# GLA decay factors: the second product in rounded parts stacked in 98 rows, both directions in one tile

## The chip, the cores and the metric

The kernel runs on one core of one Trainium2 chip, as one launch. The metric is the device time in microseconds (us) of that launch. The engines named below are PE (matrix products), ACT (functions, copies and casts), DVE (elementwise work), POOL and SP, which issues nearly all transfers. Each engine works through its own instructions in a fixed order and waits for the others by semaphores.

## The reference

The reference is one layer of a hybrid diffusion backbone, for 128 context tokens and 256 latent tokens with 2048 channels. The part that the change touches is the decay of the gated linear attention (GLA): four heads, key width 128, two directions, chunks of 64 tokens. Cut to that part:

```python
lr_f, lr_b = ...            # two slices of h @ w_in, 16 columns each
la_f = heads(jax.nn.log_sigmoid((lr_f @ lw['w_a2_fwd'] + lw['b_a_fwd']).astype(jnp.float32)) / GLA_TAU, GLA_DK)
la_b = heads(jax.nn.log_sigmoid((lr_b @ lw['w_a2_bwd'] + lw['b_a_bwd']).astype(jnp.float32)) / GLA_TAU, GLA_DK)
...
b = jnp.cumsum(lc, axis=3)                 # in a chunk, along the direction
q_in = qc * jnp.exp(b)
k_in = kc * jnp.exp(-b)
k_out = kc * jnp.exp(total - b)
```

The product with `w_a2` is called the second product here: a row of 16 low-rank factors, and a bias, give the decay logits z of a token in 512 key channels per direction. From `q_in`, `k_in` and `k_out` follow the attention inside the chunks, the running state and the outputs. Around this stand the input projections, a Fourier branch, per-channel gates, an output projection and a SwiGLU feed-forward part.

## The kernel before

All 384 tokens are handled together, T = 384 columns, with channels in the partitions. A product of full precision is made of rounded parts: each operand is split into `hi`, its rounded copy (type F32R), and `lo`, the rest, and three products hi-hi, hi-lo and lo-hi are added in PSUM (`gemm`, L249). Weights come in tiles of 128x1024 (`raw`, two buffers); a cast on ACT (L220, `whi`) and a subtraction on DVE (L221, `wlo`) split each tile, into one of four buffers. One tile serves half a projection: 24 matmuls of 384 columns. `grab` (L240) takes the oldest split tile and at once queues the load and the split of another, so three half projections lie between a split and its use. `proj` (L258) does a projection in two halves, and after each half it calls `step(side)`.

The side work of the gate stage is two generators (`side`, L761), advanced by one `yield` each after every half projection. One is `gla` (L583), the attention, head by head: 14 yields a head. The other is `ada_rest` (L519), a matrix-vector product on DVE that loads 512 KB (`adaw`) and does two instructions (`adacc`, L530) per yield. The order on PE, ACT, DVE and POOL is as written in the program; the order of SP's transfers is chosen by a scheduler.

Of a head's 14 steps the first five matter here:

- transposes of k (`kr`, L598);
- `z` of direction 0, and its logarithms;
- `z` of direction 1, and its logarithms;
- `bT` and `sx` of direction 0 (the cumulative sums, products with the triangular matrix `tri`);
- `bT` and `sx` of direction 1.

The logits z of a direction are three plain fp32 matmuls (L614) of 33 rows (32 low-rank factors of both directions, and a row of ones for the bias; the other direction's 16 rows of `a2` are zero) by 128 columns. Then log-sigmoid: ACT takes |z| (L618), exp(-|z|) (L619) and ln(1 + .) (L620), DVE subtracts that from min(z, 0) (L621), ACT rounds the result (`lah`, L624) and DVE takes the rest (`lal`, L625).

The 33-row operand `lr` is made in three moves. The first low-rank products are made in plain fp32, in four row groups (`lrprod`, L409). Those are summed by a selection matrix `sel32` (`plr`, L750), and ACT copies the 32 rows (L752). `a2` and the constants are loaded at the end of the first stage (L496, L497), into a buffer of x that is then free.

Of the kernel before, what the change touches and what calls it, by code (L numbers as in the profile page):

```python
# [11 lines left out]
F32 = mybir.dt.float32  # L12
# [8 lines left out]
P = 128  # L21
# [21 lines left out]
C_MASK = 512  # L43
C_SELS = 640
C_SELR = C_SELS + 2
C_SEL32 = C_SELR + 64
HC, HL = TC // 2 + 1, TL // 2 + 1
HT = HC + HL
C_CR = C_SEL32 + 32
C_CT = C_CR + 129 + 129 + 128  # L50
C_LT = C_CT + 2 * HC
NC = C_LT + 2 * 2 * HL
# [2 lines left out]
def _constants():  # L55
    c = np.zeros((P, NC), np.float32)
    j = np.arange(P)[:, None]
    i = np.arange(P)[None, :]
    same = (j // CH) == (i // CH)
    c[:, 0:128] = (same & (j <= i)) / TAU  # L60
    c[:, 128:256] = (same & (j >= i)) / TAU
    c[:, 256:384] = (j > i) / TAU
    c[:, 384:512] = (j < i) / TAU
    jc, ic = j % CH, np.arange(CH)[None, :]
    c[:, C_MASK : C_MASK + CH] = jc <= ic
    c[:, C_MASK + CH : C_MASK + 2 * CH] = jc >= ic
    r = np.arange(P)
    for k in range(2):
        c[:, C_SELS + k] = (r % 32) == k
        c[:, C_SELR + 32 * k + k] = 1.0  # L70
    c[:, C_SEL32 : C_SEL32 + 32] = (r[:, None] % 32) == np.arange(32)[None, :]
# [21 lines left out]
def tile_step(ctx: ExitStack, tc: tile.TileContext, a, o):  # L93
# [26 lines left out]
    sel32 = const.tile([P, 32], F32, name="sel32")  # L120
    selr = const.tile([P, 64], F32, name="selr")
    tmp1 = const.tile([P, 1], F32, name="tmp1")

# [188 lines left out]
    with ExitStack() as s:  # L312
# [38 lines left out]
        load_w(1)  # L351
        wlr = pa.tile([P, KT, 32], F32, name="wlr")
        SP.dma_start(wlr, a["w_lr"])
        SP.dma_start(sel32, a["consts"][:, C_SEL32 : C_SEL32 + 32])
# [84 lines left out]
        for kb in range(KT):  # L439
# [48 lines left out]
            if kb:  # L488
# [2 lines left out]
                pe_x(3)  # L491
                flushes[3]()
                prev = new
        cgt = actp.tile([P, 8, T], F32, tag="C_lo", name="cg")
        cg = cgt.rearrange("p a b -> p (a b)")
        SP.dma_start(cg[:, 0:640], a["consts"][:, 0:640])  # L496
        SP.dma_start(cg[0:33, 768:1792], a["a2"])  # L497
        lrmm, lrflush = lrprod(KT - 4)
        lrmm()
        lrflush(cgt[:, 6, :])  # L500
        push()
        qk = actp.tile([P, 8, T], F32, tag="C_hi", name="qk")
# [61 lines left out]

        return qk[:, h:8:4, t * P : (t + 1) * P]

    a2 = cg[0:33, 768:1792]
    rate = [1.0]
    ada_gen = ada_rest((2, 3, 4))
    ada = paced(ada_gen, rate)  # L570
    with ExitStack() as s:
        pg = s.enter_context(tc.tile_pool(name="pg", bufs=1))
        tri = pg.tile([P, 512], F32R, name="tri")
        mask = pg.tile([P, 2, CH], U32, name="mask")
        ss = pg.tile([P, 3, 4], F32, name="ss")

# [6 lines left out]
        def gla():  # L583
            def split2(tags, src):
                out = [pg.tile([P, src.shape[1], src.shape[2]], F32R, tag=t, name="part") for t in tags]
                split_act(*out, src)
                return out
# [6 lines left out]
            for h in range(NH):  # L594
# [11 lines left out]
                    SP.dma_start(s0[d], a["s0"][d, h])  # L606
                yield
                qin, kin, kcr, kout, dec = [], [], [], [], []
                lasplit = []
                for d in range(2):  # L610
                    z = pss.tile([P, 3, P], F32, tag="side", name="z")
                    for t in range(3):
                        c0 = d * 512 + h * P
                        PE.matmul(  # L614
                            z[:, t, :], lr[0:33, t * P : (t + 1) * P], a2[0:33, c0 : c0 + P], start=True, stop=True,
                        )
                    la = pg.tile([P, 3, P], F32, tag=f"la{d}", name="la")
                    ACT.activation(la, z, AF.Abs)  # L618
                    ACT.activation(la, la, AF.Exp, scale=-1.0)  # L619
                    ACT.activation(la, la, AF.Ln, bias=1.0)  # L620
                    DVE.scalar_tensor_tensor(la, z, 0.0, la, op0=ALU.min, op1=ALU.subtract)  # L621
                    lah = pg.tile([P, 3, P], F32R, tag=f"lah{d}", name="lah")
                    lal = pg.tile([P, 3, P], F32R, tag=f"lal{d}", name="lal")
                    ACT.copy(lah, la)  # L624
                    DVE.tensor_sub(lal, la, lah.bitcast(F32))  # L625
                    lasplit.append((lah, lal))
                    yield
                for d in range(2):
                    lah, lal = lasplit[d]


                    bT = pss.tile([P, T], F32, tag="side", name="bT")
                    for t in range(3):
                        for j, l in enumerate((lah, lal)):
                            PE.matmul(
                                bT[:, t * P : (t + 1) * P], l[:, t, :], tri[:, d * P : (d + 1) * P],
                                start=j == 0, stop=j == 1,
                            )
                    sx = pss.tile([P, 2, P], F32, tag="side", name="sx")
                    for j, l in enumerate((lah, lal)):  # L640
                        PE.matmul(
                            sx, tri[:, (2 + d) * P : (3 + d) * P], l[:, 0 : 2 + d : 1 + d, :], start=j == 0, stop=j == 1,
                        )
# [24 lines left out]
                    yield  # L668
# [35 lines left out]
                ap = split2(("la0", "la1"), att)  # L704
                yield
                qp = [split2((f"lah{d}", f"lal{d}"), qin[d].rearrange("p (t i) -> p t i", t=3)) for d in range(2)]
# [43 lines left out]
        PE.matmul(plr[0:32, :], sel32, cgt[:, 6, :], start=True, stop=True)  # L750
        lr = cgt[0:33, 7, :]
        ACT.copy(lr[0:32, :], plr[0:32, :])  # L752
        POOL.memset(lr[32:33, :], 1.0)
        for i in range(4):
            proj(psm, hT, keep(kT, i), ada)
        DVE.tensor_copy(tri, cg[:, 0:512])
        DVE.tensor_copy(mask, cg[:, C_MASK : C_MASK + 2 * CH].rearrange("p (a b) -> p a b", a=2))

        gl = gla()

# [549 lines left out]
```

## Time and profile before

| what | value |
|---|---|
| three timed runs | 2064.86, 2067.26, 2067.55 us; median 2067.26 |
| the profiled execution, its own time | 2063.03 us |
| its span, first to last instruction | 2061.3 us |
| mean granted clock of PE | 0.994 |
| busy: PE, DVE, ACT, POOL | 2031.1, 1273.7, 780.5, 45.4 us |
| transfers | 373.64 MB, mean 181 GB/s |

A row of a group or of the timeline names the line of the program, the engine, the operation, and `out<-in` by the names of the tiles. Rows of the timeline begin with the start and the length in microseconds; in brackets stand the idle time of the engine before the row and what ended it. PE records overlap, since matmuls are pipelined: the time that a matmul takes of PE is read from start to start. A plain fp32 matmul is recorded as two.

### The profile page before, as it was taken

How to read it: one execution, taken by the hardware profiler on the slowest of the kernel's cores; microseconds unless marked ns; L12 is line 12 of the kernel's file. 1: busy time of each engine (PE TensorE's matmuls, PEld its weight loads, DVE VectorE, ACT ScalarE, POOL GpSimd, SP SyncE). 2: the span in 40 equal slices, each digit the busy share in tenths (PEclk: the TensorE clock that was granted, in tenths of full speed). 3: DMA queues.
4: the chain of work that ended last, by engine and by line, in shares of the span. 5: the costliest groups of instructions: out<-in, count | busy, mean ns of one | idle time of the engine just before them, and what ended most of it. 6: DMA issues, size and time to landing. Idle time of an engine off the chain costs nothing.

```text
span 2061.3 us, 30173 instructions
## 1 busy us (share of the span) xinstructions
PE 2031.1 (99%) x12250; PEld 1959.8 (95%) x12250; DVE 1273.7 (62%) x1662; ACT 780.5 (38%) x1161; POOL 45.4 (2%) x52
## 2 busy tenths in 40 slices
PE   8999999999999999998999999999999999999997
PEld 5779999999999999988999999999999999999996
DVE  5669787888667787867444545453545454544346
ACT  3233555454346554445333223222222222232234
POOL 0000000000000000023000000000000000000001
PEclk9999999999999999999999999999999999999999
DMA  9977666767546685632444444443444444433332
GB/s 387 352 274 262 196 223 226 243 206 263 203 154 224 237 294 179 193 124 74 162 145 142 154 153 143 143 151 126 143 143 154 144 151 146 149 127 123 123 133 82
DMA packets 112167, 373.64 MB, mean 181 GB/s; under 512 B 13627, under 2 KB 32251, under 8 KB 107932
## 3 DMA queue, kind: packets, MB, share of 16 engines
q1 hardware_dynamic: 111164, 370.54, 52.5%
q8 instruction: 96, 1.57, 0.3%
q10 hardware_dynamic: 864, 1.18, 0.2%
q14 instruction: 43, 0.35, 0.1%
HBM read 358.04 MB, written 13.63 MB: 180 GB/s over the span
## 4 chain that ended last, share of the span: by engine, by line
PE 96%; DVE 2%; issue 0%; DMA 0%; ACT 0%; SPq 0%; DVEq 0%; ACTq 0%
PE pmm L253 66%; PE pdn L253 18%; PE pv L387 3%; PE pf L253 2%; PE pgm L370 2%; PE px L405 1%; DVE yE L1205 0%; PE po L592 0%; DMA Clo<-in_xT 0%; PE pr L538 0%; PE z L614 0%; DVE z L1068 0%; PE dl L592 0%; PE pgm L468 0%; DVE z L1062 0%
## 5 line engine op out<-in xcount | busy, mean ns | idle before, releaser
L253 PE MATMUL pmm<-A_hi,whi 128*128 128x384 f32 x2480 | 833.3, 336 | 0.0
L253 PE MATMUL pmm<-A_hi,wlo 128*128 128x384 f32 x2480 | 829.1, 334 | 0.0
L253 PE MATMUL pmm<-A_lo,whi 128*128 128x384 f32 x2480 | 829.0, 334 | 0.0
L221 DVE TENSOR_TENSOR wlo<-raw,whi 128x1024 fp32r<-128x1024 f32 x433 | 529.1, 1224 | 433.1 <-ACT whi L220 424.1
L220 ACT CAST whi<-raw 128x1024 fp32r<-128x1024 f32 x436 | 457.6, 1050 | 616.9 <-PE pmm L253 212.0
L253 PEld LDWEIGHTS pmm<-A_hi,whi 128*128 128x128 f32 x2480 | 465.6, 188 | 4.8 <-issue 1.6
L253 PEld LDWEIGHTS pmm<-A_lo,whi 128*128 128x128 f32 x2480 | 465.7, 188 | 0.0
L253 PEld LDWEIGHTS pmm<-A_hi,wlo 128*128 128x128 f32 x2480 | 465.6, 188 | 0.0
L530 DVE SCALAR_TENSOR_TENSOR adacc<-adaw,spad,adacc 128x1024 f32<-128x1024 f32 x240 | 297.0, 1279 | 0.9 <-DMA adaw<-in_w_ada 0.7
L253 PE MATMUL pdn<-hid_hi,whi 128*128 128x384 f32 x704 | 235.2, 334 | 0.0
L253 PE MATMUL pdn<-hid_hi,wlo 128*128 128x384 f32 x704 | 235.1, 334 | 0.0
L253 PE MATMUL pdn<-hid_lo,whi 128*128 128x384 f32 x704 | 235.1, 334 | 0.0
L253 PEld LDWEIGHTS pdn<-hid_hi,whi 128*128 128x128 f32 x704 | 132.2, 188 | 0.4 <-issue 0.4
L253 PEld LDWEIGHTS pdn<-hid_lo,whi 128*128 128x128 f32 x704 | 132.2, 188 | 0.0
L253 PEld LDWEIGHTS pdn<-hid_hi,wlo 128*128 128x128 f32 x704 | 132.2, 188 | 0.0
L279 ACT CAST hid_hi<-hfE 128x384 fp32r<-128x384 f32 x44 | 22.6, 513 | 160.4 <-DVE hfE L1132 160.4
L1132 DVE TENSOR_TENSOR hfE<-sg,pmm 128x384 f32<-128x384 f32 x44 | 24.4, 555 | 81.1 <-PE pmm L253 80.5
L1124 ACT ACTIVATE sg<-pmm 128x384 f32<-128x384 f32 x44 | 21.7, 492 | 133.3 <-PE pmm L253 133.3
L1149 DVE TENSOR_TENSOR Blo<-Blo,pdn 128x384 f32<-128x384 f32 x72 | 39.5, 553 | 46.6 <-PE pdn L253 46.6
L1149 DVE TENSOR_TENSOR Bhi<-Bhi,pdn 128x384 f32<-128x384 f32 x72 | 39.2, 550 | 34.1 <-PE pdn L253 33.9
L253 PE MATMUL pmm<-o_hi,whi 128*128 128x384 f32 x128 | 42.8, 335 | 0.0
L253 PE MATMUL pmm<-o_lo,whi 128*128 128x384 f32 x128 | 42.8, 334 | 0.0
(297 smaller groups left out, 1575.6 us busy)
## 6 DMA issues: line engine op xcount, KB each, us to landing
adaw<-in_w_ada SPq DMA_DIRECT2D x128, 512.0 KB
raw<-in_w_g SPq DMA_DIRECT2D x88, 512.0 KB
raw<-in_w_u SPq DMA_DIRECT2D x88, 512.0 KB
raw<-in_w_d SPq DMA_DIRECT2D x88, 512.0 KB
slab<-in_w_ada SPq DMA_DIRECT2D x32, 1024.0 KB
raw<-in_w_gate SPq DMA_DIRECT2D x64, 512.0 KB
raw<-in_w_in SPq DMA_DIRECT2D x44, 512.0 KB
raw<-in_w_out SPq DMA_DIRECT2D x32, 512.0 KB
```

The lines of the kernel that those rows point to most:

```text
L220: ACT.copy(hi, raw)
L221: eng.tensor_sub(lo, raw, hi.bitcast(F32))
L253: PE.matmul(dst, w[wi][:, k * n + n0 : k * n + n0 + P], x[xi][:, k0 + k, :], start=first and k == 0 and j == 0, stop=last and k == kts - 1 ...
L279: ACT.copy(hi, src)
L370: PE.matmul(pgv[q : q + 32, :], spad[:, k, :], slab[k // (KT // 2)][:, k % (KT // 2), :], start=k < 4, stop=k >= KT - 4,)
L387: PE.matmul(pv[2 * t + g], hT[x_][:, kb, t * P : (t + 1) * P], w_[:, g * 512 : (g + 1) * 512], start=kb == 0 and j == 0, stop=kb == KT - 1 ...
L405: PE.matmul(px, w_[:, u * P : (u + 1) * P], hT[x_][:, kb, :], start=j == 0, stop=j == 2)
L530: DVE.scalar_tensor_tensor(acc[:, c, :], w, spad[:, k, c : c + 1], acc[:, c, :], op0=ALU.mult, op1=ALU.add,)
L1124: ACT.activation(sgs[j], p, AF.Silu)
L1132: DVE.tensor_mul(hf, sgs.pop(j), p)
L1149: DVE.tensor_add(acc(k), acc(k), p)
```

## The change

- **The operands of the second product** become rounded parts. `lr` has 98 rows: 32 rows of hi, the same 32 rows again, 32 rows of lo, and two rows of ones. `a2` has 98 rows too: hi, lo, hi, then the bias as hi and lo. One matmul in F32R over 98 rows adds the three products and the bias.
- **Side by side**: the columns of `a2` are laid out by head, direction, channel, so that one matmul of 256 columns gives both directions of a head. Three matmuls a head take the place of six.
- **One tile per head** holds the decays of both directions: |z| in two instructions (512 and 256 columns, by PSUM tile), the other functions in one of 768 columns, the subtraction in two, `lah` and `lal` in one each. z of both directions stands in the second step of a head and the logarithms stand in the third. Before, each direction had its z and its logarithms in one step. The number of steps is the same.
- **Preparation**: the selection matrix gives three copies of the 32 rows (96 columns). Ten transfers (constants, selection, eight pieces of `a2`) go to the tiles of `la`, `lah` and `lal` in place of two to `cg`. Before the gate stage two ACT and four DVE instructions make the parts of `a2`; one more on DVE makes the lo rows of `lr`. `tri` moves to `cg`.

```diff
+        cg = actp.tile([P, 8 * T], F32R, tag="C_lo", name="cg")
+        tri, a2, lr = cg[:, 0:512], cg[0:98, 768:1792], cg[0:98, 7 * T : 8 * T]
+        part = pg.tile([P, 512], F32R, name="a2part")
+        raw3 = [pg.tile([P, 768], F32, tag=t, name="raw3") for t in ("la", "lah", "lal")]
+        SP.dma_start(raw3[0][:, 0:640], a["consts"][:, 0:640])
+        SP.dma_start(raw3[0][:, 640:736], a["consts"][:, C_SEL3 : C_SEL3 + 96])
+        for c in range(2):
+            src = a["a2"][:, 512 * c : 512 * c + 512]
+            for n in range(3):
+                SP.dma_start(raw3[1 + c][32 * n : 32 * n + 32, 0:512], src[0:32])
+            SP.dma_start(raw3[1 + c][96:98, 0:512], src[32:33].to_broadcast([2, 512]))
...
-                lasplit = []
+                z = [pss.tile([P, n, 2, P], F32, tag="side", name="z") for n in (2, 1)]
+                for t in range(3):
+                    PE.matmul(
+                        z[t // 2][:, t % 2], lr[:, t * P : (t + 1) * P], a2[:, h * 2 * P : (h + 1) * 2 * P],
+                        start=True, stop=True,
+                    )
+                yield
+                la = pg.tile([P, 3, 2, P], F32, tag="la", name="la")
+                lap = [la[:, 0:2], la[:, 2:3]]
+                for n in range(2):
+                    ACT.activation(lap[n], z[n], AF.Abs)
+                ACT.activation(la, la, AF.Exp, scale=-1.0)
+                ACT.activation(la, la, AF.Ln, bias=1.0)
+                for n in range(2):
+                    DVE.scalar_tensor_tensor(lap[n], z[n], 0.0, lap[n], op0=ALU.min, op1=ALU.subtract)
+                lah, lal = (pg.tile([P, 3, 2, P], F32R, tag=t, name=t) for t in ("lah", "lal"))
+                split_act(lah, lal, la)
+                yield
                 for d in range(2):
-                    z = pss.tile([P, 3, P], F32, tag="side", name="z")
-                    for t in range(3):
-                        c0 = d * 512 + h * P
-                        PE.matmul(
-                            z[:, t, :], lr[0:33, t * P : (t + 1) * P], a2[0:33, c0 : c0 + P], start=True, stop=True,
-                        )
-                    la = pg.tile([P, 3, P], F32, tag=f"la{d}", name="la")
-                    ACT.activation(la, z, AF.Abs)
-                    ACT.activation(la, la, AF.Exp, scale=-1.0)
-                    ACT.activation(la, la, AF.Ln, bias=1.0)
-                    DVE.scalar_tensor_tensor(la, z, 0.0, la, op0=ALU.min, op1=ALU.subtract)
-                    lah = pg.tile([P, 3, P], F32R, tag=f"lah{d}", name="lah")
-                    lal = pg.tile([P, 3, P], F32R, tag=f"lal{d}", name="lal")
-                    ACT.copy(lah, la)
-                    DVE.tensor_sub(lal, la, lah.bitcast(F32))
-                    lasplit.append((lah, lal))
-                    yield
-                for d in range(2):
-                    lah, lal = lasplit[d]
...
-        PE.matmul(plr[0:32, :], sel32, cgt[:, 6, :], start=True, stop=True)
-        lr = cgt[0:33, 7, :]
-        ACT.copy(lr[0:32, :], plr[0:32, :])
-        POOL.memset(lr[32:33, :], 1.0)
+        PE.matmul(plr[0:96, :], raw3[0][:, 640:736], qk[:, 7, :], start=True, stop=True)
+        ACT.copy(lr[0:96], plr[0:96, :])
+        DVE.tensor_sub(lr[64:96], plr[64:96, :], lr[64:96].bitcast(F32))
+        POOL.memset(lr[96:98].bitcast(F32), 1.0)
         for i in range(4):
             proj(psm, hT, keep(kT, i), ada)
...
+        for c in range(2):
+            dst = a2.rearrange("p (h d j) -> p d h j", d=2, j=P)[:, c]
+            raw, up = (x.rearrange("p (h j) -> p h j", j=P) for x in (raw3[1 + c][0:98, 0:512], part[0:98]))
+            ACT.copy(up, raw)
+            DVE.tensor_scalar_mul(dst, up.bitcast(F32), coef[0:98, 1:2])
+            DVE.scalar_tensor_tensor(dst, raw, coef[0:98, 0:1], dst.bitcast(F32), op0=ALU.mult, op1=ALU.add)
```

More of the change, by code (lines that the diff above doesn't have):

```diff
@@ L45 @@
 C_SELR = C_SELS + 2
-C_SEL32 = C_SELR + 64
+C_COEF = C_SELR + 64
+C_SEL3 = C_COEF + 2
 HC, HL = TC // 2 + 1, TL // 2 + 1
 HT = HC + HL
-C_CR = C_SEL32 + 32
+C_CR = C_SEL3 + 96
 C_CT = C_CR + 129 + 129 + 128
@@ L70, in _constants @@
         c[:, C_SELR + 32 * k + k] = 1.0
-    c[:, C_SEL32 : C_SEL32 + 32] = (r[:, None] % 32) == np.arange(32)[None, :]
+    rest = ((r >= 32) & (r < 64)) | (r == 97)
+    c[:, C_COEF] = rest
+    c[:, C_COEF + 1] = np.where(rest, -1, 1)
+    c[:, C_SEL3 : C_SEL3 + 96] = (r[:, None] % 32) == (np.arange(96) % 32)[None, :]
     jj = np.arange(129)[None, :]
@@ L119, in tile_step @@
     msx = const.tile([P, 3], F32, name="msx")
-    sel32 = const.tile([P, 32], F32, name="sel32")
+    coef = const.tile([P, 32], F32, name="coef")
     selr = const.tile([P, 64], F32, name="selr")
@@ L353, in tile_step @@
         SP.dma_start(wlr, a["w_lr"])
-        SP.dma_start(sel32, a["consts"][:, C_SEL32 : C_SEL32 + 32])
+        SP.dma_start(coef[:, 0:2], a["consts"][:, C_COEF : C_COEF + 2])
         SP.dma_start(bgate, a["b_gate"])
@@ L493, in tile_step @@
                 prev = new
[L494 to L497, printed above, removed]
+        qk = actp.tile([P, 8, T], F32, tag="C_hi", name="qk")
         lrmm, lrflush = lrprod(KT - 4)
         lrmm()
-        lrflush(cgt[:, 6, :])
+        lrflush(qk[:, 7, :])
         push()
-        qk = actp.tile([P, 8, T], F32, tag="C_hi", name="qk")
         vr = [actp.tile([P, 3, 1024], F32R, tag=t, name="vr") for t in ("B_hi", "B_lo")]
@@ L565, in on @@
         return qk[:, h:8:4, t * P : (t + 1) * P]
-    a2 = cg[0:33, 768:1792]
     rate = [1.0]
@@ L572, in tile_step @@
         pg = s.enter_context(tc.tile_pool(name="pg", bufs=1))
-        tri = pg.tile([P, 512], F32R, name="tri")
+        cg = actp.tile([P, 8 * T], F32R, tag="C_lo", name="cg")
[9 more added lines that the diff above has]
+            SP.dma_start(raw3[1 + c][96:98, 0:512], src[32:33].to_broadcast([2, 512]))
         mask = pg.tile([P, 2, CH], U32, name="mask")
@@ L635, in gla @@
                             PE.matmul(
-                                bT[:, t * P : (t + 1) * P], l[:, t, :], tri[:, d * P : (d + 1) * P],
+                                bT[:, t * P : (t + 1) * P], l[:, t, d], tri[:, d * P : (d + 1) * P],
                                 start=j == 0, stop=j == 1,
@@ L641, in gla @@
                         PE.matmul(
-                            sx, tri[:, (2 + d) * P : (3 + d) * P], l[:, 0 : 2 + d : 1 + d, :], start=j == 0, stop=j == 1,
+                            sx, tri[:, (2 + d) * P : (3 + d) * P], l[:, 0 : 2 + d : 1 + d, d], start=j == 0, stop=j == 1,
                         )
@@ L703, in gla @@
                 kp = [split2((f"koh{d}", f"kol{d}"), kout[d]) for d in range(2)]
-                ap = split2(("la0", "la1"), att)
+                apt = pg.tile([P, 2, 3, P], F32R, tag="la", name="ap")
+                ap = [apt[:, 0], apt[:, 1]]
+                split_act(*ap, att)
                 yield
-                qp = [split2((f"lah{d}", f"lal{d}"), qin[d].rearrange("p (t i) -> p t i", t=3)) for d in range(2)]
+                qpt = [pg.tile([P, 2, 3, P], F32R, tag=t, name="qp") for t in ("lah", "lal")]
+                qp = [[q[:, d] for q in qpt] for d in range(2)]
+                for d in range(2):
+                    split_act(*qp[d], qin[d].rearrange("p (t i) -> p t i", t=3))
                 sp = [split2((f"s0h{d}", f"s0l{d}"), s0[d]) for d in range(2)]
@@ L749, in tile_step @@
         plr = pss.tile([P, T], F32, tag="side", name="plr")
-        PE.matmul(plr[0:32, :], sel32, cgt[:, 6, :], start=True, stop=True)
-        lr = cgt[0:33, 7, :]
-        ACT.copy(lr[0:32, :], plr[0:32, :])
-        POOL.memset(lr[32:33, :], 1.0)
+        PE.matmul(plr[0:96, :], raw3[0][:, 640:736], qk[:, 7, :], start=True, stop=True)
+        ACT.copy(lr[0:96], plr[0:96, :])
+        DVE.tensor_sub(lr[64:96], plr[64:96, :], lr[64:96].bitcast(F32))
+        POOL.memset(lr[96:98].bitcast(F32), 1.0)
         for i in range(4):
             proj(psm, hT, keep(kT, i), ada)
-        DVE.tensor_copy(tri, cg[:, 0:512])
-        DVE.tensor_copy(mask, cg[:, C_MASK : C_MASK + 2 * CH].rearrange("p (a b) -> p a b", a=2))
+        DVE.tensor_copy(tri, raw3[0][:, 0:512])
+        DVE.tensor_copy(mask, raw3[0][:, C_MASK : C_MASK + 2 * CH].rearrange("p (a b) -> p a b", a=2))
+        for c in range(2):
[4 more added lines that the diff above has]
+            DVE.scalar_tensor_tensor(dst, raw, coef[0:98, 0:1], dst.bitcast(F32), op0=ALU.mult, op1=ALU.add)
         gl = gla()
```

## The prediction

> **What bounds the kernel now.** I read the page first: span, busy shares, the chain that ended last.
>
> ```profile
> span 2061.3 us, 30173 instructions
> PE 2031.1 (99%) x12250; PEld 1959.8 (95%) x12250; DVE 1273.7 (62%) x1662; ACT 780.5 (38%) x1161; POOL 45.4 (2%) x52
> PE 96%; DVE 2%; issue 0%; DMA 0%; ACT 0%; SPq 0%; DVEq 0%; ACTq 0%
> ```
>
> TensorE is nearly always busy and carries 96% of the chain, so time taken off PE's stream shortens the span unless a new wait fills the hole. The change lies in the gate stage, 203 to 481 us, so I asked for the windows next, then for the waits between 140 and 440 us.
>
> ```profile
> 203.00:481.00 278.00, 278.00 (x1794) 269.11 (x1792) 227.44 (x293) 145.15 (x251) 1.86 (x6) 1.00 0.68 222
> ACT whi L220 <- DMA raw<-in_w_gate: 45.7, 17, 4.7
> ```
>
> The window's columns are length, then busy time of PE, PEld, DVE, ACT and POOL, then granted clock, DMA share, GB/s. PE is busy for all 278 us at full clock: no helper work of the attention heads makes it wait today. DVE is busy 227 of 278 us, ACT 145. ACT's largest wait here is for weight tiles; it matters below because a cast of such a tile comes to stand ahead of the decay work.
>
> **Part 1: the second product on PE.** The timeline of PE, the start of each row first:
>
> ```profile
> 203.70 0.33 PE L253 MATMUL pmm<-A_hi,whi 128*128 128x384 f32 x1
> ...
> 207.16 0.34 PE L253 MATMUL pmm<-A_hi,wlo 128*128 128x384 f32 x1
> 207.43 0.93 PE L614 MATMUL z<-cg 33*128 33x128 f32 x6
> ...
> 208.75 0.33 PE L253 MATMUL pmm<-A_hi,wlo 128*128 128x384 f32 x1
> ```
>
> From 203.70 to 207.16 lie 20 steps of the projection: 3.46 / 20 = 0.173 us each. From 207.16 to 208.75 are 1.59 us, of which three steps (0.52) are projection, so one z block costs PE 1.07 us: three plain fp32 matmuls, each recorded as two, and a slow return to the rounded stream. There are two per head and four heads, together 8.56 us.
>
> The new block is three matmuls per head of 256 columns in rounded fp32 with 98 rows. The trace has none with 98 rows; the nearest is a po block, the same type, width and count with 128 rows:
>
> ```profile
> 257.66 0.34 PE L253 MATMUL pmm<-A_hi,wlo 128*128 128x384 f32 x1
> 257.83 0.52 PE L592 MATMUL po<-vr,part 128*128 128x256 f32 x3
> 258.19 0.34 PE L253 MATMUL pmm<-A_hi,whi 128*128 128x384 f32 x1
> ```
>
> 0.53 less one step is 0.36 us. The far bounds are twice that row (0.72) and the old cost of both directions (2.14, no gain); I take 0.36, since only the row count differs. Saved: 4 x (2.14 - 0.36) = 7.1 us.
>
> The selection product plr keeps its two fp32 passes but loads 96 columns instead of 32:
>
> ```profile
> L750 PEld LDWEIGHTS plr<-cg,sel 128*32 128x32 f32 x2 | 0.1, 108 | 0.2 <-issue 0.2
> L614 PEld LDWEIGHTS z<-cg 33*128 33x128 f32 x48 | 5.9, 187 | 2.0 <-issue 2.0
> ```
>
> Two loads grow by at most 187 - 108 = 79 ns: 0 to 0.16 us, I take 0.1. The other matmuls (bT, sx, at, po) keep count, width and type. PE's own gain is 7.0 us.
>
> **Part 2: the chain from z to the cumulative sums.** Before, z of direction 0, z of direction 1, bT of 0 and bT of 1 stand in four successive steps, a step being half a projection (24 matmuls). The logarithms of a direction are made in the step of its z, so two half projections lie between them and their bT. The built order of the new kernel has z of both in the first step, the logarithms of both in the second, bT of 0 in the third: two half projections cover a chain twice as wide. In ACT's order the chain now also stands behind the weight cast (whi, L220) of the next half projection, where it stood ahead of it. ACT and DVE, head 0 before:
>
> ```profile
> 207.54 0.58 ACT L772 ACTIVATE gz<-pmm,bgate 128x384 f32<-128x384 f32 x1 [2.74 <-PE pmm L253]
> 208.40 0.49 ACT L618 ACTIVATE la<-z 128x384 f32<-128x384 f32 x1 [0.28 <-PE z L614]
> 208.91 1.28 ACT L619 ACT_TABLE_LOAD   x1
> 210.20 0.53 ACT L619 ACTIVATE la<-la 128x384 f32<-128x384 f32 x1
> 210.75 1.28 ACT L620 ACT_TABLE_LOAD   x1
> 212.04 0.53 ACT L620 ACTIVATE la<-la 128x384 f32<-128x384 f32 x1
> 213.19 0.51 ACT L624 CAST lah<-la 128x384 fp32r<-128x384 f32 x1 [0.62 <-DVE la L621]
> 213.61 1.05 ACT L220 CAST whi<-raw 128x1024 fp32r<-128x1024 f32 x1
> ```
>
> ```profile
> 212.60 0.56 DVE L621 SCALAR_TENSOR_TENSOR la<-z,la 128x384 f32<-128x384 f32 x1 [6.54 <-ACT la L620]
> 213.74 0.56 DVE L625 TENSOR_TENSOR lal<-la,lah 128x384 fp32r<-128x384 f32 x1 [0.58 <-ACT lah L624]
> ```
>
> Widths by slope: on ACT a cast goes from 0.51 us (384) to 1.05 (1024), 0.84 ns a column; on DVE 0.56 (384) to 1.28 (1024), 1.13 ns a column by the first row below.
>
> ```profile
> L530 DVE SCALAR_TENSOR_TENSOR adacc<-adaw,spad,adacc 128x1024 f32<-128x1024 f32 x93 | 115.2, 1279 | 0.4 <-DMA adaw<-in_w_ada 0.2
> 278.37 0.49 ACT L618 ACTIVATE la<-z 128x384 f32<-128x384 f32 x1 [0.28 <-PE z L614]
> 278.90 0.53 ACT L619 ACTIVATE la<-la 128x384 f32<-128x384 f32 x1
> ```
>
> The last two rows are head 1: there the exponential follows the absolute value with no table load, so heads 1 to 3 pay one load, head 0 two. In the new order, from the start of the last projection matmul before z (207.16 in head 0) as zero: gz starts at 0.38; whi at 0.86 (successive instructions overlap by 0.1); absolute value of 512 columns at 1.82 (0.60), of 256 at 2.32 (0.39), ending at 2.71; exponential of 768 (0.53 + 384 x 0.84 ns = 0.85) 2.74 to 3.59; load to 4.88; logarithm to 5.74; on DVE two subtractions (0.70 and 0.42) to 6.8; cast lah (0.84) 6.83 to 7.67; lal (0.56 to 1.0; I take 0.96) to 8.65. PE comes to bT this way:
>
> ```profile
> 217.67 0.34 PE L253 MATMUL pmm<-A_hi,wlo 128*128 128x384 f32 x1
> 217.85 0.22 PE L635 MATMUL bT<-tri,lah 128*128 128x128 f32 x1
> 217.91 0.27 PE L635 MATMUL bT<-tri,lal 128*128 128x128 f32 x1
> ```
>
> bT's second matmul, which reads lal, stands 0.24 us behind the last projection matmul: 0.36 + 48 x 0.173 + 0.24 = 8.91. In heads 1 to 3 the operand is there at 8.65, a quarter of a microsecond ahead; I put 0.1 us of stall on each (0 to 0.4). In head 0 the second load adds 1.28: ready at 9.93, or up to 0.4 later where whi's tile lands late (below): a stall of 1.0 to 1.6, I take 1.4. Together 1.7 us. Queued behind the waiting bT on PE is the whole stream of projections; nothing runs past it.
>
> The Trainium skill (page "ScalarE: Activation LUTs", section "What ACT_TABLE_LOAD costs") speaks against this margin: a switch costs the 1283 ns load plus about 1380 ns of drain. Here the load of 210.75 starts 0.02 us after the exponential ended and the logarithm starts 0.01 us after the load, so the trace shows no drain. By the page the chains would be 1.38 us longer for each load, two in head 0 and one in the others, the stall 4.2 + 3 x 1.2 = 7.8 in place of 1.7, and the gain gone; by the row the sum stands.
>
> Hidden elsewhere: eight table loads go, on an engine that is half idle. DVE loses five small instructions and no longer sits 6.54 us ahead of the first subtraction, since two adacc and a wlo now stand before it; they end near 3.2 on the scale above, before the 5.77 at which it is wanted. The preparation of a2 (two ACT copies of 512 columns near 0.6; four DVE instructions near 0.4 to 0.7; 2.4 us on DVE) falls at 199 us in front of weights that PE wants two or three half projections later; if that cover were gone it would cost those 2.4 us. The 0.56 us at most that lo of lr takes on DVE at 165 us is hidden the same way.
>
> **Part 3: the queue of SP at the start.** Two loads become ten: constants, selection, eight pieces of a2. They stand ahead of the fourth half projection's weights.
>
> ```profile
> 144.26 0.33 SPq L192 DMA_DIRECT2D raw<-in_w_in  x1
> 149.46 7.18 SPq L192 DMA_DIRECT2D raw<-in_w_in  x3
> ...
> 135.79 1.58 SPq L497 DMA_DIRECT2D cg<-in_a  x1
> L851 SPq DMA_DIRECT2D wr<-in_w_br_four x24: 620/621/737, 520.9 to 545.4; - x24
> 153.97 1.05 ACT L220 CAST whi<-raw 128x1024 fp32r<-128x1024 f32 x1 [4.46 <-DMA raw<-in_w_in]
> 164.50 0.83 PE L750 MATMUL plr<-cg,sel 128*32 128x384 f32 x2
> 166.17 0.33 SPq L192 DMA_DIRECT2D raw<-in_w_in  x1
> 171.04 1.06 ACT L220 CAST whi<-raw 128x1024 fp32r<-128x1024 f32 x1 [3.18 <-DMA raw<-in_w_in]
> ```
>
> An issue takes 0.33 us for a full tile, 0.62 or 1.58 for odd shapes: nine of them stand behind the third weights' issue (144.26 to 144.6) and take 3.0 to 14 us; I take 0.6 each, so SP is free at 150.0. The fourth weights went out at 149.46, when their buffer came free, and would now be 0.5 us late. Their cast, at 153.97, feeds the half projection that ends before plr at 164.50, so begins near 160.2; with the low part (1.28) it is ready at 156.3, 3.9 us early. Hidden: nothing.
>
> The last two rows give 4.9 us from issue to cast of a tile that was waited for. The casts that now lead the chains have their tiles issued well ahead:
>
> ```profile
> 201.59 0.33 SPq L192 DMA_DIRECT2D raw<-in_w_gate  x1
> 271.96 0.33 SPq L192 DMA_DIRECT2D raw<-in_w_gate  x1
> ```
>
> Wanted at 208.0 and 278.0, that is 6.4 and 6.0 us later. In head 0 the a2 preparation eats up to 2 us of that, hence the 0.4 above.
>
> **Sum.** 7.1 - 0.1 - 1.7 = 5.3 us less. The profiled execution took 2063.03 us (span 2061.3 and 1.7 around it), so 2057.7; the median of the three runs, 2067.26, lies 4.2 above it, so I forecast 2062.0 us.
>
> **The rivals.**
> *The margin is lost in every head.* A quarter of a microsecond is all that heads 1 to 3 have. If wide instructions, semaphores and the weight load of lal together cost 1.1 to 1.6 us more in each head, the stall is 5 to 7 and the time 2065 to 2067. For it: all terms add up in one chain. Against: all but three widths are rows. 0.20.
> *A table switch holds ACT for longer than its load.* Taken as a second load's time, 1.28 us, the operand is ready at 9.93 in heads 1 to 3 (stall 1.1 each) and head 0 stalls 1.4 + 2.56: together 7.3, time 2067.6. The rows at 210.75 and 212.04 speak against it. 0.03. This is the mechanism of the Trainium skill's "ScalarE: Activation LUTs", weighed above.
> *SP's queue starves the start.* If the new issues take the 14 us, the fourth weights come 9 us late, 3.9 of them covered: PE waits about 5 and the time is 2067. For: the 1.58 row. Against: only two of the nine have an odd row count. 0.07.
> *Slower: the cast that leads the chain waits for its tile.* ACT runs in order, so the decay chain would sit behind a DMA. The wait row gives 45.7 / 17 = 2.7 us each. At that price in all four heads the stall is 1.7 + 10.8 = 12.5, the time 2067.26 + 5.5 = 2072.8. It cancels the gain from 1.3 us a head on. For: this stage has 17 such waits. Against: the 6 us of lead. 0.08.
>
> **How the numbers follow.** The forecast has 0.62 and spans 2060 (no stall) to 2063.5. A measurement can tell about 0.2%, 4.1 us, so the forecast lies just beyond that line; of its 0.62 I give 0.06 to "within". Faster 0.56; within 0.2%: 0.06 + 0.20 + 0.03 + 0.07 = 0.36; slower 0.08. The range reaches from 2058 (no stall, less the 2.4 us by which the lowest of the three runs, 2064.86, lies under the median) to 2067.5 (first three rivals), and leaves the slower one out.
>
> **What would show it.** Right: z rows x3 per head with about 0.36 us between projection matmuls; a wait of PE for lal of 1 to 1.6 us at the first head and almost none at the others; eight table loads fewer. Wrong: a PE wait at bT above 1 us in later heads (the chain's widths), whi of the same step waiting for raw (the slower rival), or a PE wait between 155 and 165 us (SP's queue).

## The result, and the profile after

| | before | after |
|---|---|---|
| median of six runs | 2064.64 us (2062.56 to 2067.55) | 2056.55 us (2055.73 to 2057.66) |
| the profiled execution | 2063.03 us | 2056.04 us |

The ratio is 0.9962, with a 95% interval of 0.9953 to 0.9972: the changed kernel is faster by 8.1 us. That is on the side that was forecast, but 1.45 us below the low end of the range. The two profiled executions differ by 7.0 us, where the sum said 5.3.

The page of the kernel after: span, busy time, the chain that ended last.

```profile
span 2054.3 us, 30097 instructions
PE 2024.7 (99%) x12214; PEld 1956.1 (95%) x12214; DVE 1274.9 (62%) x1663; ACT 770.1 (37%) x1143; POOL 45.4 (2%) x52
PE 96%; DVE 2%; DMA 1%; ACT 1%; issue 0%; SPq 0%; DVEq 0%; ACTq 0%
```

PE bounds the kernel as before. Its busy time fell by 6.4 us, with 36 records fewer: z went from 48 records to 12. ACT lost 10 us and 18 instructions, and nobody waited for that.

The timeline of PE around z at head 0:

```profile
206.85 0.33 PE L257 MATMUL pmm<-A_hi,wlo 128*128 128x384 f32 x1
207.02 0.52 PE L623 MATMUL z<-cg 98*128 98x256 f32 x3
207.38 0.34 PE L257 MATMUL pmm<-A_hi,whi 128*128 128x384 f32 x1
```

From 206.85 to 207.38 are 0.53 us; less one step, z of both directions costs 0.36 us, the number taken from the po row. The other three heads have the same block.

Head 0's decays on ACT, then on DVE, then PE where it meets them:

```profile
207.22 0.58 ACT L794 ACTIVATE gz<-pmm,bgate 128x384 f32<-128x384 f32 x1 [2.73 <-PE pmm L257]
207.70 1.04 ACT L224 CAST whi<-raw 128x1024 fp32r<-128x1024 f32 x1
208.64 0.87 ACT L631 ACTIVATE la<-z 128x512 f32<-128x512 f32 x2
209.53 1.28 ACT L632 ACT_TABLE_LOAD   x1
210.82 0.85 ACT L632 ACTIVATE la<-la 128x768 f32<-128x768 f32 x1
211.69 1.28 ACT L633 ACT_TABLE_LOAD   x1
212.98 0.85 ACT L633 ACTIVATE la<-la 128x768 f32<-128x768 f32 x1
214.97 0.83 ACT L283 CAST lah<-la 128x768 fp32r<-128x768 f32 x1 [1.14 <-DVE la L635]
```

```profile
213.87 1.02 DVE L635 SCALAR_TENSOR_TENSOR la<-z,la 128x512 f32<-128x512 f32 x2 [3.61 <-ACT la L633]
215.84 0.96 DVE L284 TENSOR_TENSOR lal<-la,lah 128x768 fp32r<-128x768 f32 x1 [0.95 <-ACT lah L283]
```

```profile
215.53 0.34 PE L257 MATMUL pmm<-A_hi,wlo 128*128 128x384 f32 x1
215.86 0.33 PE L645 MATMUL bT<-cg,lah 128*128 128x128 f32 x1
216.85 0.33 PE L645 MATMUL bT<-cg,lal 128*128 128x128 f32 x1 [0.67 <-DVE lal L284]
...
217.75 0.34 PE L257 MATMUL pmm<-A_hi,whi 128*128 128x384 f32 x1
```

The cast whi follows gz at once, with no wait for its tile. lal is ready at 216.80, 9.95 us after the last projection matmul before z; the forecast was 9.93. PE waits for it. From 215.53 to 217.75 are 2.22 us, so the block of bT and sx takes 2.05 us over a projection step. Where nothing waits it takes 0.91 (in the kernel before, 217.67 to 218.75): the stall is 1.14 us. At head 1 the operand is there in time:

```profile
283.86 0.96 DVE L284 TENSOR_TENSOR lal<-la,lah 128x768 fp32r<-128x768 f32 x1 [0.95 <-ACT lah L283]
285.06 0.27 PE L645 MATMUL bT<-cg,lal 128*128 128x128 f32 x1
```

It ends at 284.82, and its reader starts at 285.06 without a wait: a quarter of a microsecond of room, as forecast. In the waits of PE between 203 and 480 us head 0's is the only one:

```profile
PE bT L645 <- DVE lal L284: 0.7, 1, 0.7
```

Set side by side at fixed landmarks on PE, the two executions divide the 7.0 us like this:

| stretch | before | after | difference | forecast |
|---|---|---|---|---|
| first step of the projections to first kr (plr in it) | 55.11 | 54.76 | -0.35 | +0.1 |
| first kr to last po (gate stage) | 274.82 | 268.61 | -6.21 | -5.4 |
| last po to first product of the Fourier part | 57.64 | 57.19 | -0.45 | 0 |
| from there to the end | 1525.95 | 1525.93 | 0.0 | 0 |

The gate stage is z with the ten projection steps behind each block, -7.3 (8.8 us in eight blocks before, 1.5 in four after), and the stall, +1.1. The other two stretches weren't foreseen. For the first, the weight loads of PE (PEld) before, then after; `issue` in brackets means that the profile shows nothing that the engine waited for:

```profile
164.07 0.19 PEld L253 LDWEIGHTS pmm<-A_hi,wlo 128*128 128x128 f32 x1
164.50 0.14 PEld L750 LDWEIGHTS plr<-cg,sel 128*32 128x32 f32 x2 [0.25 <-issue]
165.27 0.19 PEld L253 LDWEIGHTS pmm<-A_hi,whi 128*128 128x128 f32 x1 [0.62 <-ACT qk L745]
```

```profile
164.10 0.19 PEld L257 LDWEIGHTS pmm<-A_hi,wlo 128*128 128x128 f32 x1
164.27 0.34 PEld L765 LDWEIGHTS plr<-qk,raw 128*96 128x96 f32 x2
164.77 0.19 PEld L257 LDWEIGHTS pmm<-A_hi,whi 128*128 128x128 f32 x1 [0.16 <-issue]
```

The load of 96 columns starts as soon as the one ahead has ended, under the running matmul. The load of 32 columns starts 0.25 us after the one ahead has ended, and the load behind it 0.62 us after that. The wide load takes longer, and the block is shorter.

For the third stretch, the transfers that SP issues (SPq), then DVE, then PE after the change:

```profile
511.81 0.33 SPq L808 DMA_DIRECT2D cd<-in_consts  x1
513.33 8.06 SPq L873 DMA_DIRECT2D wr<-in_w_br_four  x12
521.49 2.10 SPq L196 DMA_DIRECT2D raw<-in_w_in  x2
```

```profile
526.54 1.23 DVE L225 TENSOR_TENSOR wlo<-raw,whi 128x1024 fp32r<-128x1024 f32 x1 [6.79 <-ACT whi L224]
527.68 0.54 DVE L898 TENSOR_TENSOR fs<-fs,pmm 128x384 f32<-128x384 f32 x1
528.33 0.67 PE L844 MATMUL px<-cd,fs 128*128 128x257 f32 x2 [1.34 <-issue]
```

SP issues twelve small pieces (wr), 8.06 us, ahead of a weight tile (raw); its split on DVE (wlo) stands ahead of the subtraction that PE needs. PE idles for 1.34 us; before it idled for 1.81.

### The profile page after: what moved, and what is told of

It reads as the page before. It is cut to its first block, busy times and chain, and to the rows that moved or that the text cites. A ratio compares the mean times of both kernels' runs of the same rounds, so it can differ in the third digit from the quotient of the medians.

```text
span 2054.3 us, 30097 instructions
## 1 busy us (share of the span) xinstructions
PE 2024.7 (99%) x12214; PEld 1956.1 (95%) x12214; DVE 1274.9 (62%) x1663; ACT 770.1 (37%) x1143; POOL 45.4 (2%) x52
## 4 chain that ended last, share of the span: by engine, by line
PE 96%; DVE 2%; DMA 1%; ACT 1%; issue 0%; SPq 0%; DVEq 0%; ACTq 0%
PE pmm L257 66%; PE pdn L257 18%; PE pv L391 3%; PE pf L257 2%; PE pgm L374 1%; PE px L409 1%; DVE yE L1227 0%; PE po L603 0%; PE pmm L1131 0%; DMA Clo<-in_xT 0%; PE pr L538 0%; DMA slab<-in_w_ada 0%; DVE z L1090 0%; PE dl L603 0%; PE px L844 0%
```

## The experiments

**The theory** was: PE's own price of z (number type, rows, two directions apart), less one extra table load at head 0, and small gains at the two ends. **Rivals**: the chain of decays is short of time in more than head 0; the gain belongs to one part of the change alone; the gains at the ends come from elsewhere.

**1. The exponential's table before the first head.**

```diff
+        ACT.activation(tmp1, eps_t, AF.Exp)
         gl = gla()
```

> The changed kernel with one more ACT instruction, an exponential of one column, ahead of the gate stage, so that head 0 finds the exponential's table loaded. Theory: the one wait of PE in the gate stage (1.14 us more in the bT block of head 0: 2.05 in place of 0.91 us) comes from the second table load in head 0's chain (1.28 us). Then the block falls to 0.91 us, as in heads 1 to 3, and the span by 1.1 us against the changed kernel's 2054.3. Rival: head 0 waits because its chain starts late (the a2 preparation, a late weight tile); then the block stays near 2.0 us and nothing is gained.

Measured: 2055.2 us (median of four executions), ratio to before 0.9952 (0.9935 to 0.9969), span 2053.2. ACT at head 0:

```profile
208.77 0.87 ACT L631 ACTIVATE la<-z 128x512 f32<-128x512 f32 x2
209.68 0.85 ACT L632 ACTIVATE la<-la 128x768 f32<-128x768 f32 x1
210.54 1.28 ACT L633 ACT_TABLE_LOAD   x1
```

One load stands in the chain in place of two, head 0's bT block falls from 2.05 to 0.91 us like the others, and no wait of PE is left in the stage. From first kr to last po it gains 1.15 us, the whole stall. The stall was one table load, and nothing else was late.

**2. The table evicted in the other heads.**

```diff
                 ACT.copy(krs, kr)
+                if h:
+                    ACT.activation(tmp1, eps_t, AF.Sqrt)
```

> The changed kernel with a square root of one column at the start of heads 1 to 3, which puts the exponential's table out, so that their chains too pay two loads. Theory: heads 1 to 3 have 0.25 us of room before bT (lal ends at 284.82, its reader is due at 285.07 in head 1), so 1.28 us more make each wait about 1.0 us: bT blocks of 1.9 to 2.0 us in all four heads, 3.1 us more in the span. Rival: the room is larger than the timeline shows; the blocks stay at 0.91 to 1.3 us and the span grows by less than 1 us.

Measured in one execution: 2062.84 us, span 2061.0. The waits of PE in the gate stage:

```profile
PE bT L647 <- DVE lal L284: 2.7, 4, 0.7
```

All four heads now have a bT block of 2.06 us, and the gate stage is 3.4 us longer: 1.15 in each of three heads, which is one load (1.28) less the room of 0.25, and 0.1 for the late start. (Of the 6.7 us in the span, 2.6 come from the start of the execution, told below, and 0.7 from the start of the Fourier part.) So the lost margin of the first rival begins a quarter of a microsecond further on: what a head's chain takes beyond that is paid for almost in full.

**3. The logarithms back in the step of z.**

```diff
-                yield
                 la = pg.tile(...)
...
                 split_act(lah, lal, la)
                 yield
+                yield
```

> The changed kernel with the logarithms of both directions moved up into the step of their z; an empty step follows, so that every other place stays. Theory: the chain's order behind the weight cast costs it 0.95 us; ahead of the cast it starts about 0.7 us earlier (it then waits for z itself), so head 0's bT block falls from 2.05 to about 1.3 us, and heads 1 to 3 stay at 0.91: 0.7 us gained. Rival: DVE then waits for the chain with two adacc and a wlo queued behind it (6.5 us of idling in the kernel before), weight tiles come late and PE waits at a projection: nothing gained, or up to 2 us lost.

Measured: 2060.45 us (median of eight executions), ratio to before 0.9976 (0.9965 to 0.9986). That is 3.9 us above the changed kernel's median; the kernel before ran 0.9 us higher in this series, and the two profiled executions differ by 3.7. The waits of PE in the gate stage:

```profile
PE dl L603 <- DVE part L284: 1.1, 3, 0.4
```

Head 0's stall fell to 0.2 us (0.4 was expected). Instead PE waits for `part` of the state product dl, where nothing waited before: its blocks are 1.8 us longer in all, so the gate stage is 0.9 us longer. At head 1 DVE works without a gap from 303.45 to 314.6 us, with `part` behind two adacc and a wlo; ACT's waits for weight tiles came to 90.1 us in this stage, against 49.2 in the changed kernel. Which of them put DVE late isn't settled. The idle time at the start of the Fourier part grew to 2.61 us, and behind it PE ran at half clock for 3.41 us: the stretch from there to the next landmark (the product pn) took 73.5 us in place of 72.1. The order in which the logarithms have a step of their own thus is not only a risk for bT: it spares the 1.8 us at dl.

**4. The stacked parts alone, one direction at a time.** Six matmuls of 128 columns, logarithms of each direction in the step of its z:

```diff
-                for t in range(3):
-                    PE.matmul(z[t // 2][:, t % 2], lr[...], a2[:, h * 2 * P : (h + 1) * 2 * P], ...)
+                for d in range(2):
+                    for t in range(3):
+                        PE.matmul(z[:, t, :], lr[...], a2[:, (2 * h + d) * P : (2 * h + d + 1) * P], ...)
```

> The changed kernel's 98-row operands alone: z again per direction (three matmuls of 128 columns each), and its logarithms in the same step in a tile of 384 columns, as in the kernel before. Theory: the stacked rounded operands carry nearly all the gain and the rest is a trade. Each z block should take 0.33 us or a little more (bT's rounded matmuls of 128 columns come every 0.11 us), two a head, so 0.3 to 0.4 us a head more than the 0.354 of one wide block: 1.2 to 1.6 us lost; head 0's wait of 1.14 us goes. Span within 0.5 us of the changed kernel's. Rival: matmuls of 128 columns in rounded fp32 run no faster than plain ones; then z blocks stay near 1 us and most of the 7.1 us are lost.

Measured in one execution: 2061.26 us, span 2059.5. A z block costs 0.34 us, 0.68 a head in place of 0.36, and z with the steps behind it 1.5 us more in all. The stall of bT is gone (-1.14), but the waits of dl that experiment 3 showed are here too (+1.8), and the gate stage is 2.2 us longer. I had expected half a microsecond: the waits of dl belong to the order in which a direction's logarithms stand with its z. Why the kernel before, in that order, has none wasn't tried; ACT's waits for weight tiles come to 72.2 us here and to 59.0 there, which doesn't settle it.

**5. The number type alone, and 6. the row count alone.**

```diff
-  z[...], lr[:, t * P : (t + 1) * P], a2[:, h * 2 * P : (h + 1) * 2 * P],
+  z[...], lr[:, t * P : (t + 1) * P].bitcast(F32), a2[:, h * 2 * P : (h + 1) * 2 * P].bitcast(F32),
```

```diff
-  z[...], lr[:, t * P : (t + 1) * P], a2[:, h * 2 * P : (h + 1) * 2 * P],
+  z[...], lr[0:33, t * P : (t + 1) * P], a2[0:33, h * 2 * P : (h + 1) * 2 * P],
```

> The changed kernel with one edit: z reads the same 98 stacked rows as plain fp32 instead of rounded fp32, still three matmuls of 256 columns per head. It takes the number type alone back. Theory (the number type is most of z's price, since a plain fp32 matmul is two passes at a slower pace): the z block of a head grows from 0.35 us over a projection step to about 1.6 us, so the gate stage is about 5 us longer and the span near 2059. Rival (the narrow 33-row operand, whose weight load is not brought in ahead, was most of it): the block stays below 1.0 us and the gate stage grows by less than 2.6 us.

> The changed kernel with z over the first 33 of its 98 rows, in rounded fp32 (two of the three products and the bias are left out). It changes the row count of the operand alone. Theory (a weight load over few rows is not brought in under the running matmul): the z block of a head grows from 0.35 us to 0.6 or 0.7 us, 1.0 to 1.4 us in all four. Rival (rows do not matter, the old price was the number type alone): the block stays at 0.35 us within 0.03.

Measured in one execution each: 2060.14 us (span 2058.4) and 2057.13 us (span 2055.3). The second kernel leaves out two of the three products and the bias, so it serves for its times alone. PE at z in plain fp32, then in rounded fp32 over 33 rows, and the weight loads of the latter:

```profile
206.94 0.33 PE L257 MATMUL pmm<-A_hi,wlo 128*128 128x384 f32 x1
207.11 1.46 PE L623 MATMUL z<-cg 98*128 98x256 f32 x6
208.22 0.53 PE L257 MATMUL pmm<-A_hi,whi 128*128 128x384 f32 x1
208.58 0.34 PE L257 MATMUL pmm<-A_lo,whi 128*128 128x384 f32 x1
```

```profile
206.85 0.34 PE L257 MATMUL pmm<-A_hi,wlo 128*128 128x384 f32 x1
207.12 0.62 PE L623 MATMUL z<-cg 33*128 33x256 f32 x3
207.68 0.44 PE L257 MATMUL pmm<-A_hi,whi 128*128 128x384 f32 x1
207.96 0.34 PE L257 MATMUL pmm<-A_lo,whi 128*128 128x384 f32 x1
```

```profile
207.12 0.41 PEld L623 LDWEIGHTS z<-cg 33*128 33x128 f32 x3 [0.25 <-issue]
```

In plain fp32 there are six records, and the second projection matmul comes late too: 206.94 to 208.58 less two steps is 1.29 us, against 0.36. My 1.6 was too high, as the rival's 1.0 was too low. Over four heads, with the steps behind the blocks, the type costs 3.85 us; the gate stage grew by only 2.9, because a longer z also gives the decays more time, and head 0's stall fell to 0.2. With 33 rows the load waits for 0.25 us as plr's of 32 columns did: 206.85 to 207.96 less two steps is 0.76 us, 0.40 more per head, 1.6 in all, above the 1.0 to 1.4 that I expected. Here too the stall shrank, by 0.4.

So of z's 7.3 us the number type has 3.85, the rows 1.6, and the two directions in one matmul 1.5, each taken back by itself. Together 6.95: close to the whole, with no part that makes the others needless.

The Trainium skill (page "TensorE: Matmul & The Clock Gate", section "LDWEIGHTS (loading the stationary operand)") has the columns, and not the rows, set how long a weight load takes. The lengths agree: the mean was 187 ns for 33 rows at z before, and is 190 ns for 128 rows at bT after. What the 33 rows cost here is not the length of the load but its start, 0.25 us late, and of that no run here shows a reason. Each block of three loads waits once, at its first load (four waits in twelve loads; eight in 48 in the kernel before).

**7. 96 columns of the selection matrix in the kernel before.**

```diff
-        PE.matmul(plr[0:32, :], sel32, cgt[:, 6, :], start=True, stop=True)      # sel32 is 128 x 32
+        PE.matmul(plr[0:96, :], sel32, cgt[:, 6, :], start=True, stop=True)      # sel32 is 128 x 96
```

> The kernel before with one edit: the selection matrix has 96 columns (three copies of the 32), so plr has 96 columns of weights in place of 32. Theory (the load of 32 columns by itself is what is not brought in ahead): the plr block falls from 0.97 us over a projection step to about 0.65 as in the changed kernel, the time is otherwise that of the kernel before. Rival (the gain at plr in the changed kernel comes from the other tile that it reads, or from what stands around it): the block stays at 0.97 us.

Measured in one execution: 2064.45 us, with a start 1.3 us later than that of the profiled execution before. The weight loads:

```profile
165.34 0.19 PEld L253 LDWEIGHTS pmm<-A_hi,wlo 128*128 128x128 f32 x1
165.52 0.34 PEld L750 LDWEIGHTS plr<-cg,sel 128*96 128x96 f32 x2
166.01 0.19 PEld L253 LDWEIGHTS pmm<-A_hi,whi 128*128 128x128 f32 x1 [0.16 <-ACT whi L220]
```

The idle 0.25 us is gone, and the block is 0.65 us, as expected, in place of 0.97. From the first step of the projections to the first kr it takes 54.78 us, as in the changed kernel (54.76; before 55.11). So the column count did it, and not the other tile.

**8. The small pieces issued by ACT, and 9. by POOL.**

```diff
-                    SP.dma_start(wr[r : r + 1, :].rearrange(...), src.rearrange(...))
+                    ACT.dma_start(wr[r : r + 1, :].rearrange(...), src.rearrange(...))
```

> The changed kernel with one edit: the 24 small transfers of the branch weights (wr) are issued by ACT's queue in place of SP's. Theory (PE's idle time at the start of the Fourier part, 1.81 us before and 1.34 us after the change, is set by SP, which issues these pieces one by one ahead of or between the tiles that DVE waits for): the idle time falls to under 0.3 us and the span by about 1 us. Rival (it is set by the release of the buffer, or by the transfer itself): the idle time stays within 0.3 us of 1.34; or ACT, held by the issues, comes late to a cast and PE idles elsewhere.

Measured in one execution: 2060.19 us, span 2058.4. ACT and the transfers that it issues (ACTq):

```profile
514.50 9.43 ACTq L873 DMA_DIRECT2D wr<-in_w_br_four  x12
523.97 2.00 ACT L224 CAST whi<-raw 128x1024 fp32r<-128x1024 f32 x2 [9.01 <-DMA wr<-in_w_br_four]
```

The rival on ACT was right: now the casts stand 9 us behind the pieces, PE idles for 3.57 us instead of 1.34, and then runs at half clock for 3.4 us. The second version has POOL in place of ACT, and experiment 1's line:

> The changed kernel with two edits: the early exponential of the run that showed no stall at the first head, and the 24 small wr transfers issued by POOL, which has almost nothing to do, in place of SP. Theory (the in-order issuer of these pieces delays the weight tile that DVE's low part waits for, 8.1 us on SP, 9.4 us on ACT; on an engine that issues nothing else they delay nobody): PE's idle time at the start of the Fourier part falls from 1.34 us to under 0.4, and the span from 2053.2 to about 2052. Rival (the gate store or the tile's buffer sets that start, whoever issues the pieces): the idle time stays at 1 us or more and the span at 2053. Second rival: POOL issues so slowly that wn is late for its product, and PE idles later in the Fourier part.

Measured: 2053.85 us (median of five executions, 2053.07 to 2054.64), ratio to before 0.9945 (0.9932 to 0.9959). POOL, and PE at the start of the Fourier part:

```profile
514.18 4.28 POOL L874 DMA_DIRECT2D wr<-in_w_br_four  x8 [0.31 <-POOL wr L869]
```

```profile
526.91 0.34 PE L257 MATMUL pmm<-A_hi,wlo 128*128 128x384 f32 x1
527.09 0.59 PE L845 MATMUL px<-cd,fs 128*128 128x257 f32 x2
```

PE goes from one to the other in a step of 0.18 us: the idle time is gone. This execution's start was 1.3 us later than experiment 1's, so the span is 2052.8; from the first kr to the end it takes 1848.9 us, against 1850.6 in experiment 1 and 1851.7 in the changed kernel. It is the best version run. Its interval still touches that of the changed kernel (0.9953 to 0.9972); the landmarks, 2.8 us, are the firmer evidence.

## Why the prediction came out as it did

**The mechanism was right.** PE bounds, the gain is z's time on PE, the price is a wait for lal at head 0 by one extra table load. z was forecast at 7.1 us, and the z blocks by themselves give that (8 x 1.07 less 4 x 0.36); some 0.2 us more lie in the projection steps around them. The chain's end at head 0 was 0.02 us off, the room at head 1 0.01 us. Eight table loads went: the lines of the exponential and the logarithm had 13 before and have 5 after. DVE did not lose the five instructions that the prediction named: the heads lose four and the preparation adds five (1662 before, 1663 after), and nothing hung on it.

One part of it was luck. The prediction took 0.36 us for z "since only the row count differs" from the po row, as if rows didn't matter. They do: 98 rows cost what 128 do, but 33 rows cost 0.40 us more per head (experiment 6).

**Three terms of the sum were mis-sized, all to the same side.**

- *The stall*, 1.7 forecast, 1.14 measured. I had added 0.4 for a late tile at head 0, which came in time, and 0.1 in each other head, where 0.25 us of room left no stall at all. What the chain itself gave, 9.93 against 8.91, was 1.0.
- *plr*, +0.1 forecast, -0.35 measured. I priced the wider load by its length. The time lay in the gaps around the narrow one, 0.25 and 0.62 us, which the timeline of the weight loads showed and the group's mean (108 ns) did not. The group row of the same line held "0.2 <-issue 0.2", and z's "2.0 <-issue 2.0": the hint was quoted, and not read.
- *The start of the Fourier part*, nothing forecast, -0.45 measured. This is the weakest gain: over nine kernels with the pieces on SP the idle time lies between 1.2 and 2.6 us, while 4.8 to 5.4 us pass from SP's issue of the last gate store to that of cd, and 15.9 to 16.9 from there to PE's first product. When SP comes to that store moves against PE from kernel to kernel; that the change itself made it earlier is not shown.

These three are 1.5 us. With them and the 0.2 around the z blocks, 5.3 becomes 7.0, the difference of the profiled executions.

**The step that failed is the last of the sum: the shift to the median of three.** All terms were read from the profiled execution of 2063.03 us, and set against it the sum gave 2057.7, 1.15 above what was measured. I then put the sum under the median of three runs, 2067.26, two of which were high. Six runs gave 2064.64, and all 27 timed executions of the kernel before that are on record have a median of 2064.86 (2062.54 to 2068.79). That is 2.6 of the 5.45 us by which the forecast was off; 1.7 are the three terms and the steps around z; the other 1.1 is the difference between the medians' gap and the profiled pair's. The base scatters at the start of the program, in every kernel. The stretch from 4 to 32 us (length, busy time of PE, PEld, DVE, ACT and POOL, granted clock, DMA share, GB/s) in the changed kernel, then in experiment 2:

```profile
4.00:32.00 28.00, 23.79 (x146) 14.17 (x146) 16.67 (x40) 13.66 (x29) 0.00 (x0) 0.94 1.02 406
```

```profile
4.00:32.00 28.00, 24.61 (x120) 14.27 (x121) 13.63 (x35) 12.01 (x26) 0.00 (x0) 0.76 1.02 406
```

PE ran at half clock for 3.4 us in the first and for 13.65 in the second, has 120 matmuls done in place of 146, and comes to the first projection step at 147.8 and 150.4 us. The half-clock stretch can be placed by finer windows: its length is 3.41, 6.83, 10.24 or 13.65 us in the profiled executions, one to four times the same length. Other executions lie between: 6.8 us at half clock cost nothing (147.7 in the kernel before), 10.2 us cost 1.3 (experiment 7). That such starts made two of the three runs high is argued, since only profiled executions show their start. The range's low end, 2058.0, rested on the same base: the sum without any stall set against 2063.03 gives 2056.0, and the measured 2056.55 lies above that. It would have held the result, though for the wrong reason: the stall was there, and the gains at the two ends made up for it.

**The rivals.** *The margin lost in every head* did not happen; experiment 2 shows what it would have cost (3.4 us) and experiment 1 that no other lateness was hidden. *A table switch that holds ACT longer* did not happen: the exponential starts 0.01 us after its load (209.53 + 1.28 to 210.82), so the drain of about 1380 ns that the Trainium skill states (page "ScalarE: Activation LUTs", section "What ACT_TABLE_LOAD costs") is not in this trace. A load added to each chain cost 1.15 us a head (experiment 2); load and drain by the page's figures, less the room of 0.25, would be an estimated 2.4. *SP's queue*: the nine issues took 4.34 us, the fourth weights went out at 149.49 in place of 149.46, and PE did not wait. *Slower, the cast that leads the chain waits for its tile*: in all four heads whi starts where gz lets it.

## What to carry to other kernels

Price a matmul block from start to start around it, with the gaps of its weight loads: at plr a longer load made a shorter block, which no mean duration shows. Set a sum of differences against the execution that it was read from, and take a shift to another base only as a spread, not as part of the forecast. When a chain meets its reader with a quarter of a microsecond to spare, one table load decides; one line that loads the table early bought back all of the stall, and small transfers belong on an engine whose queue holds nothing that the critical path needs.

## What the runs showed of the hardware

- Behind loads of 128 rows and columns, a load of 32 columns, or of 33 rows, started 0.25 us late; loads of 96 columns and of 98 rows didn't (experiments 6 and 7). The wait stands at the change, not at every narrow load: in the first stage of the changed kernel the product pgm has 512 loads of 32 columns, in groups of 32, and only 21 waits. The reason stays open.
- Twelve small transfers hold their issuer for 8.06 us on SP and 9.43 on ACT; on POOL the issues took 6.5 us in all (experiments 8 and 9).
- PE came back at half clock after an idle time of 2.61 us (experiment 3) and 3.57 (experiment 8), and not after 2.45 (experiment 5): the granted clock from 528 to 535 us was 0.76, 0.76 and 1.00. The Trainium skill (page "TensorE: Matmul & The Clock Gate", section "HAM oscillation — how this bites in real kernels") puts the limit near 3.4 us; here 2.61 was enough. The length of the idle time alone doesn't decide: the clock fell 2.3 us after PE's last matmul in experiment 3 and 3.1 us after it in experiment 8, and had not fallen after 2.45 in experiment 5.
